# An FFN's last output group: its weights moved into activation room, four norms moved behind the loop, and residual rows queued behind chunks

## The chip, the cores and the metric

The kernel runs on one core of one Trainium2 chip. The metric is the device time of one execution in microseconds, lower is better. The time given is the median of several runs.

## The reference

Two layers over a sequence of 1024 positions with 1024 channels, all in float32. Layer 0 mixes tokens with a state-space model and a gated linear unit, layer 1 with a short gated convolution. Each layer then has a dense SwiGLU FFN and an embedding that is gated by the residual stream:

```python
h = x
for i in range(2):
    hn = rmsnorm(h, norm_mix_g[i])
    mix = s5_mixer(hn, ...) if i % 2 == 0 else shortconv_mixer(hn, ...)
    h = h + mix
    h = h + swiglu_ffn(rmsnorm(h, norm_ffn_g[i]), ffn_w_in[i], ffn_w_out[i])
    gate = sigmoid(rmsnorm(h, norm_ple_g[i]) @ ple_w_gate[i])
    h = h + gate * (p[i] @ ple_w_up[i])
return rmsnorm(h, final_norm_g)
```

The FFN's hidden width is 2816, which is 22 pieces of 128. `swiglu_ffn` is `(silu(gate) * up) @ w_out` with `gate, up` from `u @ w_in`.

## The kernel before, in words

The sequence is cut into 8 tiles `t` of 128 positions. Each product of two float32 matrices is made from three products of a rounded high part and a low part (`mm3`, lines 121 to 124): high by high, high by low, low by high. `split` (lines 86 to 88) makes the two parts, the high one with a cast on ScalarE (ACT), the low one with a subtract on VectorE (DVE). A weight piece or an activation tile thus fills two parts of a room.

The rooms are: `ulow`, which is cut in four quarters `q`, each with two weight rooms (`slot_low(q, s)`), or the normed activations of tiles `q` and `q + 4` (`act_view`); `uhigh` with six weight rooms (`slot_high(i)`); and the tile pool `s8` with four more (`slot_new(i)`), two of which also serve as the place of a normed row `xn` in `norm_tile`. Everything that is loaded from memory and then split or multiplied goes through four raw slots of 512 KB, `r0` to `r3`, taken in turn by `raw_tile`: raw weights, chunks of hidden activations and, where norms come in pairs, normed rows.

The FFN's first half, `ffn_in`, writes the hidden activations to memory (`hid`). Its second half is `ffn_out`, which lists a room for each of the 22 pieces of the output weights, cuts them into three groups of 8, 8 and 6, and calls `out_phase`. `out_phase` also makes the convolution's output product (`conv_out`, two groups of four pieces). Its work:

- Group 0's weights are fetched ahead. Then, group by group, all tiles follow in the order 0, 4, 1, 5, 2, 6, 3, 7 (`ORDER`).
- For each tile the chunks of hidden activations are loaded on the queue of the sync engine (SP), four pieces to a chunk (line 346). In group 0 the tile's residual row `h[t]`, 512 KB, is loaded there too (line 348).
- For each half of the 1024 output columns, each piece has three matmuls of 512 columns. A tile has 48 in a group of 8 pieces, 36 in a group of 6, 24 in the convolution. The sum is added to `h[t]` on DVE (line 360); in the last group its square sum is taken on ACT (line 139).
- After a tile, one fetch of the next group's weights is made if its room is free already (the flag that stands with the room). Fetches whose room is still in use are made after the whole loop. In the last group the fetches are those of the gate's weights (`ple_units`).
- In the last group `last_post(t)` follows the tile. In an FFN that is `norm_tile`: norm, 8 transposes on TensorE, and two splits into the tile's place in `ulow`. For the convolution it is the function in `posted` that calls `norm_pair(q)` for tiles `q` and `q + 4`, pair 0 after tile 1, pair 1 after tile 2, pair 2 after tile 3, pair 3 after tile 7, and spills the rows to memory on the queue of GpSimd (POOL). A pair is two multiplies (line 173), 16 transposes (line 181), four differences and seven splits.

After an FFN's output stage comes `ple`, the gate: two halves of the columns, each over all tiles in the same order, 24 matmuls a tile. After the convolution's output stage comes the second FFN's `ffn_in`, whose first product takes the first block of all four pairs.

The instructions of each engine are put in order by a planner when the program is built. It goes by the order in which the program is written, among what its own model finds ready; `first()` raises a few instructions by 100 places. On the chip each engine and queue runs its list in that order.

Of the kernel before, what the change touches and what calls it, by code (L numbers as in the profile page):

```python
# [9 lines left out]
F32 = mybir.dt.float32  # L10
# [13 lines left out]
def trunk(  # L24
# [7 lines left out]
    nc = tc.nc  # L32
# [31 lines left out]
    HT = T // 2  # L64
# [4 lines left out]
    h, hpool = {}, None  # L69
# [9 lines left out]
    hdram = dram.tile([T, P, D], F32, name="hd")  # L79
    hid = [dram.tile([T, P, 4, 2, P], F32, name=f"hid{i}") for i in range((NHT + 3) // 4)]  # L80

    def psum(pool=None):
        pool = pool or mm
        return pool.tile([P, 512], F32, name="ps" + pool.name, tag="ps")
# [7 lines left out]
    def raw_tile(i=None, shape=(P, D), dt=F32, name="raw"):  # L92
        if i is None:
            slots.append(slots.pop(0))
        tag = slots[-1] if i is None else f"r{i}"
        return (uhp if tag == "r3" else rawp).tile(list(shape), dt, name=name, tag=tag)

    def load_raw(src, pattern, **kw):
        raw = raw_tile()
        nc.sync.dma_start(out=raw.rearrange(pattern, **kw), in_=src)  # L100
        return raw


    def slot_low(q, s):
        v = ulow[:, q, s * 2 * D:(s + 1) * 2 * D].rearrange("p (l n) -> p l n", l=2)
        return v[:, 0], v[:, 1]

    def slot_high(i):
        v = uhigh.rearrange("p c k l j -> p (c k l j)")[:, i * 2 * D:(i + 1) * 2 * D].rearrange("p (l n) -> p l n", l=2)
        return v[:, 0], v[:, 1]  # L110
# [5 lines left out]
    def unit_of(slot, raw):  # L116
        hi, lo = slot
        split(hi, lo, raw)
        return hi, lo

    def mm3(ps, ahi, alo, bhi, blo, start, stop, more=False):
        PE.matmul(ps, ahi, bhi, start=start, stop=False, skip_group_check=more)  # L122
        PE.matmul(ps, ahi, blo, start=False, stop=False, skip_group_check=more)  # L123
        PE.matmul(ps, alo, bhi, start=False, stop=stop, skip_group_check=more)  # L124
# [4 lines left out]
    def first():  # L129
        return tc.high_priority(offset=100)  # L130

    def square(t, cs):

        if "ms" not in squares:
            squares["ms"] = tiny.tile([P, T, 4], F32, name="ms", tag="ms")
        got = squares.setdefault(t, [])
        junk = t2_tile("junk", BF16, D)
        ms = squares["ms"][:, t, len(got):len(got) + 1]
        A.activation(junk[:, cs], h[t][:, cs], AF.Square, scale=1.0 / math.sqrt(D), accum_out=ms)  # L139
        got.append(ms)  # L140
# [13 lines left out]
    def load_gain(g_row):  # L154
        gb = tiny.tile([P, D], F32, name="gb", tag="gb")
        nc.gpsimd.dma_start(out=gb, in_=g_row.partition_broadcast(P))
        return gb
# [49 lines left out]
    def norm_pair(q, gb):  # L207
        t0, t1 = q, q + HT
        halves = 2 if q == HT - 1 else 1
        x0, x1 = normed(t0, gb, halves), normed(t1, gb, halves)  # L210

        def put(c, src):
            split(moving_part(c, 0, q), moving_part(c, 1, q), by_kt(src))

        p11, p12, p22 = transposed(x0, 0), transposed(x1, 0), transposed(x1, 1)
        p21 = transposed(x0, 1, mm)
        put(0, p11)
        b12 = t2_tile("b12")
        A.copy(b12, p12)
        T1 = t2_tile("T1")  # L220
        V.tensor_tensor(T1, b12, p11, ALU.subtract)
        T2 = t2_tile("T2")
        V.tensor_tensor(T2, p22, T1, ALU.subtract)
        put(1, T2)
        put(2, T1)
        put(3, p21)
        T3 = t2_tile("T3")
        V.tensor_tensor(T3, p22, b12, ALU.subtract)
        put(4, T3)
        put(5, p22)  # L230
        T4 = t2_tile("T4")
        V.tensor_tensor(T4, p21, T2, ALU.subtract)
        put(6, T4)
# [92 lines left out]
    def out_phase(wout, groups, last_post, following=()):  # L326


        def fetch(ht, room):
            return unit_of(room(), load_raw(wout[ht], "p n -> p n"))  # L330

        units = {ht: fetch(ht, room) for ht, room, _ in groups[0]}
        for gi, group in enumerate(groups):
            last = gi == len(groups) - 1
            todo = [(early, lambda ht=ht, room=room: units.__setitem__(ht, fetch(ht, room)))
                    for ht, room, early in ([] if last else groups[gi + 1])]
            todo = todo or list(following)
            soon, late = [f for early, f in todo if early], [f for early, f in todo if not early]
            for t in ORDER:
                parts = {}  # L340
                for ht, *_ in group:
                    if ht // 4 not in parts:
                        parts[ht // 4] = ch = raw_tile(shape=(P, 4, 2, P), dt=F32R, name="ch")
                        of = [x[0] % 4 for x in group if x[0] // 4 == ht // 4]
                        ks = slice(min(of), max(of) + 1)
                        nc.sync.dma_start(out=ch[:, ks].bitcast(F32), in_=hid[ht // 4][t, :, ks])
                if gi == 0:
                    nc.sync.dma_start(out=h[t], in_=hdram[t])
                ps = [psum() for _ in range(2)]
                for j in parts:  # L350
                    mine = [x[0] for x in group if x[0] // 4 == j]
                    for nb in range(2):
                        cs = slice(nb * 512, (nb + 1) * 512)
                        for ht in mine:
                            ch = parts[j][:, ht % 4]
                            bhi, blo = (w[:, cs] for w in units[ht])
                            mm3(ps[nb], ch[:, 0], ch[:, 1], bhi, blo, ht == group[0][0], ht == group[-1][0])
                        if mine[-1] == group[-1][0]:
                            with first():
                                V.tensor_tensor(h[t][:, cs], ps[nb], h[t][:, cs], ALU.add)  # L360
                                if last:
                                    square(t, cs)
                if soon:
                    soon.pop(0)()
                if last:
                    last_post(t)
            for f in soon + late:
                f()

    def room_low(q, s):  # L370
        return lambda: slot_low(q, s)

    def room_high(i):
        return lambda: slot_high(i)

    def room_new(i):
        return lambda: slot_new(i)
# [18 lines left out]
    def ffn_out(l, post, following):  # L396
        rooms = [(room_low(q, s), False) for s in range(2) for q in range(HT)]
        rooms += [(room_high(i), True) for i in range(6)] + [(room_new(i), True) for i in range(4)]
        rooms += [(room_high(i), False) for i in range(4)]
        hts = [(ht, *room) for ht, room in enumerate(rooms)]  # L400
        cuts = [0, 8, 16, NHT]
        out_phase(ffn_w_out[l].rearrange("(ht p) n -> ht p n", p=P), [hts[a:b] for a, b in zip(cuts, cuts[1:])], post,
                  following)

    def ple_units(l, nb, rooms):

        wg = ple_w_gate[l].rearrange("(kt p) n -> p kt n", p=P)
        units = {}

        def fetch(u):  # L410
            raw = load_raw(wg[:, 2 * u:2 * u + 2, nb * 512:(nb + 1) * 512], "p (kt n) -> p kt n", kt=2)
            units[u] = [a.rearrange("p (kt n) -> p kt n", kt=2) for a in unit_of(rooms[u](), raw)]

        return units, [lambda u=u: fetch(u) for u in range(KT // 2)]
# [595 lines left out]
    def posted(gain, pairs):  # L1010

        gb = load_gain(gain)

        def pair(q):
            norm_pair(q, gb)
            spill(q)
            spill(q + HT)

        def post(t):
            if not pairs:  # L1020
                return norm_tile(t, gb)
            if 0 < t < HT:
                pair(t - 1)
            if t == T - 1:
                pair(HT - 1)
        return post
# [17 lines left out]
        h_tiles()  # L1044

    def ffn_ple(l, last):
        units, makers = ple_units(l, 0, [room_high(i) for i in (4, 5, 0, 1)])
        ffn_out(l, posted(norm_ple_g[l], False), [(i < 2, f) for i, f in enumerate(makers)])
        if last:
            gb = load_gain(final_norm_g)  # L1050
            ple(l, units, lambda t: final_tile(t, gb))
        else:
            ple(l, units, posted(norm_mix_g[l + 1], True))
# [46 lines left out]
```

## Time and profile before

| | us |
|---|---|
| median of 3 runs (2353.3 to 2358.04) | 2356.06 |
| the profiled execution | 2359.43 |
| its span, first to last instruction | 2357.5 |
| PE busy | 2247.0 (95%) |
| DVE busy | 1331.9 (56%) |
| ACT busy | 765.5 (32%) |
| POOL busy | 163.1 (7%) |
| mean granted clock of TensorE | 0.981 |

PE is TensorE's matmuls, PEld its weight loads, L346 is line 346 of the kernel. In a row of waits stand what waited, for what, the total in us, how often, and the longest. In a row of the timeline stand start, length, engine, line, operation, out<-in, shape and count, and in brackets the idle time before it with what ended it. In a row of the chain stand start, length and what was on it. Matmuls overlap, so one that the timeline shows with 0.39 us leaves room for the next after some 0.23. In the stage order of the span: state-space mixer and gated unit to about 420 us, first FFN's first half to 848, its output stage to 1113, gate to 1226, convolution's first half to about 1460, its output stage to 1557, second FFN's first half from 1571 to 1998, its output stage to 2260, last gate and final norm to the end.

### The profile page before, as it was taken

The page shows a single profiled execution, that of the slowest core. Times are in us where ns is not written, and L with a number is a line of the kernel's source. Part 1 is how long each engine was busy: PE and PEld are TensorE (multiplying, and loading weights), DVE is VectorE, ACT ScalarE, POOL GpSimd, SP SyncE. Part 2 cuts the span into 40 slices and gives each one's busy share as a digit, 9 for nine tenths or more (in the row PEclk, how much of TensorE's full clock was granted, in tenths as well). Part 3 has the DMA queues.
Part 4 walks back from the last instruction along what each step waited for, and adds up shares of the span by engine and source line. Part 5 has one row for each costly group of instructions (what it writes and reads, how often), then busy time and mean ns, then how long its engine had stood idle before and what let it go on. Part 6 is the DMA issues. An engine that isn't in the chain of part 4 may idle for free.

```text
span 2357.5 us, 27090 instructions
## 1 busy us (share of the span) xinstructions
PE 2247.0 (95%) x10253; PEld 1835.7 (78%) x10253; DVE 1331.9 (56%) x2246; ACT 765.5 (32%) x1449; POOL 163.1 (7%) x268
## 2 busy tenths in 40 slices
PE   6888999899999999999979999989999999999998
PEld 4776887788888878878858888768888888788787
DVE  7785326866666642125488776487666666121454
ACT  6554223433333320013343332153333333000232
POOL 2110001000000000000000000010000001000000
PEclk8999999999999999999989999999999999999999
DMA  7555202333333364333232225434333335543333
GB/s 246 141 135 148 69 1 89 105 112 112 111 114 110 107 241 149 118 127 114 70 129 81 90 92 179 159 125 125 108 108 107 111 113 172 212 139 107 108 109 110
DMA packets 212978, 288.87 MB, mean 123 GB/s; under 512 B 21360, under 2 KB 152432, under 8 KB 212848
## 3 DMA queue, kind: packets, MB, share of 16 engines
q1 hardware_dynamic: 191520, 212.63, 29.0%
q0 software_dynamic: 20928, 74.47, 10.2%
q8 instruction: 80, 1.31, 0.2%
q14 instruction: 50, 0.41, 0.1%
q10 hardware_dynamic: 400, 0.04, 0.0%
HBM read 190.93 MB, written 79.69 MB: 115 GB/s over the span
## 4 chain that ended last, share of the span: by engine, by line
PE 85%; DMA 6%; DVE 5%; ACT 1%; SPq 1%; issue 1%; POOL 0%; DVEq 0%; POOLq 0%; ACTq 0%
PE psmm L122 27%; PE psmm L124 27%; PE psmm L123 27%; DMA ch<-hid 2%; PE pstr L181 1%; DMA raw<-in_ffn_w_out_dram 1%; DMA tw<-tmp 1%; DVE W L575 1%; DVE gv L925 1%; DMA h<-hd 1%; DVE tmp L575 1%; DVE ulow L88 1%; DVE uhigh L88 1%; PE pstr L874 0%; DVE raw L575 0%
## 5 line engine op out<-in xcount | busy, mean ns | idle before, releaser
L122 PE MATMUL psmm<-ulow,ws 128*128 128x512 f32 x896 | 351.1, 393 | 1.6 <-ACT s L301 1.6
L123 PE MATMUL psmm<-ulow,ws 128*128 128x512 f32 x896 | 350.6, 391 | 0.0
L124 PE MATMUL psmm<-ulow,ws 128*128 128x512 f32 x896 | 350.4, 391 | 0.0
L124 PE MATMUL psmm<-uhigh,ws 128*128 128x512 f32 x672 | 265.3, 395 | 0.0
L122 PE MATMUL psmm<-uhigh,ws 128*128 128x512 f32 x672 | 265.1, 394 | 0.0
L123 PE MATMUL psmm<-uhigh,ws 128*128 128x512 f32 x672 | 264.9, 394 | 0.0
L360 DVE TENSOR_TENSOR h<-psmm,h 128x512 f32<-128x512 f32 x128 | 88.0, 690 | 276.6 <-PE psmm L124 276.6
L88 DVE TENSOR_TENSOR ws<-raw,ws 128x512 fp32r<-128x512 f32 x224 | 153.6, 688 | 117.8 <-ACT ws L87 117.4
L87 ACT CAST ws<-raw 128x512 fp32r<-128x512 f32 x224 | 137.5, 619 | 213.0 <-PE psmm L124 211.2
L122 PEld LDWEIGHTS psmm<-ulow,ws 128*128 128x128 f32 x896 | 169.4, 189 | 39.5 <-ACT s L301 2.9
L123 PEld LDWEIGHTS psmm<-ulow,ws 128*128 128x128 f32 x896 | 169.4, 189 | 36.2
L124 PEld LDWEIGHTS psmm<-ulow,ws 128*128 128x128 f32 x896 | 169.2, 189 | 36.2
L87 ACT CAST ws<-st 128x512 fp32r<-128x512 f32 x168 | 104.0, 620 | 204.4 <-PE psmm L124 189.5
L123 PEld LDWEIGHTS psmm<-uhigh,ws 128*128 128x128 f32 x672 | 126.1, 188 | 30.3
L124 PEld LDWEIGHTS psmm<-uhigh,ws 128*128 128x128 f32 x672 | 126.1, 188 | 30.3
L122 PEld LDWEIGHTS psmm<-uhigh,ws 128*128 128x128 f32 x672 | 126.1, 188 | 29.1
L323 POOL DMA_DIRECT2D hid<-hs x104 | 78.2, 755 | 903.4 <-DVE hs L88 895.4
L122 PE MATMUL psmm<-ulow,ch 128*128 128x512 f32 x320 | 128.4, 401 | 10.8 <-DMA ch<-hid 10.8
L139 ACT ACTIVATE junk<-h 128x512 bf16<-128x512 f32 (+1 forms) x113 | 64.0, 567 | 204.0 <-DVE h L360 104.0
L87 ACT CAST uhigh<-raw 128x1024 fp32r<-128x1024 f32 x36 | 37.2, 1049 | 278.9 <-PE psmm L124 136.7
L123 PE MATMUL psmm<-ulow,ch 128*128 128x512 f32 x320 | 127.6, 399 | 0.0
L124 PE MATMUL psmm<-ulow,ch 128*128 128x512 f32 x320 | 127.5, 398 | 0.0
(240 smaller groups left out, 4238.5 us busy)
## 6 DMA issues: line engine op xcount, KB each, us to landing
hid<-hs POOLq DMA_DIRECT2D x104, 512.0 KB, 4.3
ch<-hid SPq DMA_DIRECT2D x96, 512.0 KB, 3.7
raw<-in_ffn_w_in_dram SPq DMA_DIRECT2D x88, 512.0 KB, 4.4
raw<-in_ffn_w_out_dram SPq DMA_DIRECT2D x44, 512.0 KB, 3.6
hd<-h POOLq DMA_DIRECT2D x24, 512.0 KB, 3.0
h<-hd SPq DMA_DIRECT2D x24, 512.0 KB, 8.7
raw<-in_conv_w_in_dram SPq DMA_DIRECT2D x24, 512.0 KB, 4.0
up<-ev SPq DMA_DIRECT2D x32, 256.0 KB, 3.2
```

Source lines behind the costliest of these rows:

```text
L87: A.copy(hi, src)
L88: V.tensor_tensor(lo, src, hi.bitcast(F32), ALU.subtract)
L122: PE.matmul(ps, ahi, bhi, start=start, stop=False, skip_group_check=more)
L123: PE.matmul(ps, ahi, blo, start=False, stop=False, skip_group_check=more)
L124: PE.matmul(ps, alo, bhi, start=False, stop=stop, skip_group_check=more)
L139: A.activation(junk[:, cs], h[t][:, cs], AF.Square, scale=1.0 / math.sqrt(D), accum_out=ms)
L181: PE.transpose(pt[:, c * P:(c + 1) * P], xn[:, kt * P:(kt + 1) * P], ident)
L323: nc.gpsimd.dma_start(out=hid[ht // 4][half * HT:(half + 1) * HT, :, ht % 4].rearrange("t p l j -> p t l j"), in_=hs.bitcast(F32))
L360: V.tensor_tensor(h[t][:, cs], ps[nb], h[t][:, cs], ALU.add)
L575: V.tensor_tensor(o, a, b, op)
L925: V.tensor_tensor_scan(gv[:, g, 1:P], dec, sv[:, g, 1:P], 0.0, ALU.mult, ALU.add)
```

## The change

There are four edits.

1. In group 0, a residual row's load is tied behind the last chunk load of its tile in the queue of SP (`tc.issue_after`). This holds for both FFNs and the convolution.
2. The last four of the FFN's 22 weight pieces go to the low rooms of quarters 2 and 3 in place of `slot_high(0..3)`. Group 0 has left these rooms before group 1 begins, so all six fetches of the last group are marked early.
3. Since these rooms are also the place of the normed tiles 2, 6, 3 and 7, the last group calls `last_post` only for tiles 0, 4, 1 and 5; the other four follow after all groups, in the same order. The test stands in `out_phase`, so it holds for the convolution too: pair 0 stays after tile 1, pairs 1, 2 and 3 follow after the loop.
4. The gate's four weight units go to `slot_high(0..3)` in place of 4, 5, 0, 1, and all four are marked early.

```diff
         units = {ht: fetch(ht, room) for ht, room, _ in groups[0]}
+        kept = []
         for gi, group in enumerate(groups):
...
-                        nc.sync.dma_start(out=ch[:, ks].bitcast(F32), in_=hid[ht // 4][t, :, ks])
+                        load = nc.sync.dma_start(out=ch[:, ks].bitcast(F32), in_=hid[ht // 4][t, :, ks])
                 if gi == 0:
-                    nc.sync.dma_start(out=h[t], in_=hdram[t])
+                    with tc.issue_after(load.ins):
+                        nc.sync.dma_start(out=h[t], in_=hdram[t])
...
-                if last:
+                if last and t % HT < HT // 2:
                     last_post(t)
+                elif last:
+                    kept.append(t)
             for f in soon + late:
                 f()
+        for t in kept:
+            last_post(t)
...
         rooms += [(room_high(i), True) for i in range(6)] + [(room_new(i), True) for i in range(4)]
-        rooms += [(room_high(i), False) for i in range(4)]
+        rooms += [(room_low(q, s), True) for q in (2, 3) for s in range(2)]
...
-        units, makers = ple_units(l, 0, [room_high(i) for i in (4, 5, 0, 1)])
-        ffn_out(l, posted(norm_ple_g[l], False), [(i < 2, f) for i, f in enumerate(makers)])
+        units, makers = ple_units(l, 0, [room_high(i) for i in range(4)])
+        ffn_out(l, posted(norm_ple_g[l], False), [(True, f) for f in makers])
```

## The prediction

> **What bounds the kernel now.** I read the page first, then the waits of the matmul engine, then a table of stretches, and last the queue of the sync engine and the chain of work at each place where the table showed lost time.
>
> ```profile
> span 2357.5 us, 27090 instructions
> PE 85%; DMA 6%; DVE 5%; ACT 1%; SPq 1%; issue 1%; POOL 0%; DVEq 0%; POOLq 0%; ACTq 0%
> ch<-hid SPq DMA_DIRECT2D x96, 512.0 KB, 3.7
> h<-hd SPq DMA_DIRECT2D x24, 512.0 KB, 8.7
> ```
>
> TensorE is the bound: 85% of the chain that ended last is its work. A change that removes no matmul can win only where TensorE stands still. Its waits say where that is.
>
> ```profile
> PE pstr L181 <- DVE xn L173: 36.0, 5, 10.7
> PE psmm L122 <- DMA ch<-hid: 19.9, 7, 4.6
> ```
>
> Two waits matter: transposes that wait for a normed row (36.0 us in 5 waits, at the ends of stages that norm pairs) and matmuls that wait for a chunk of hidden activations (19.9 us in 7). The change touches the second, and, through the convolution's output stage, the first.
>
> The next rows are stretches of the span. After the length come busy time and instructions of PE, PEld, DVE, ACT and POOL, the granted clock, and DMA share and GB/s.
>
> ```profile
> 848.02:880.00 31.98, 27.39 (x109) 21.81 (x109) 9.23 (x12) 3.33 (x5) 2.05 (x3) 0.89 0.80 301
> 880.00:1030.00 150.00, 150.00 (x653) 122.49 (x652) 30.57 (x37) 10.40 (x10) 0.00 (x0) 1.00 0.38 126
> 1036.00:1054.00 18.00, 13.23 (x45) 9.86 (x44) 6.52 (x8) 4.48 (x7) 0.56 (x1) 0.81 0.42 145
> 1112.59:1158.09 45.50, 45.50 (x201) 37.00 (x200) 20.13 (x33) 16.76 (x32) 2.12 (x2) 1.00 0.32 104
> 1465.00:1485.00 20.00, 17.27 (x73) 13.38 (x72) 8.68 (x12) 4.17 (x5) 1.65 (x3) 1.00 0.89 326
> 1485.00:1523.00 38.00, 38.00 (x164) 30.58 (x163) 13.32 (x21) 3.34 (x9) 2.24 (x4) 1.00 0.35 119
> 1557.15:1571.31 14.16, 3.44 (x25) 3.10 (x23) 11.32 (x20) 6.50 (x14) 1.44 (x2) 0.73 0.48 149
> 1997.65:2029.00 31.35, 27.90 (x114) 22.16 (x113) 8.00 (x11) 3.36 (x5) 2.06 (x3) 0.95 0.79 303
> 2184.00:2202.00 18.00, 13.21 (x48) 10.01 (x47) 6.51 (x8) 4.48 (x7) 0.56 (x1) 0.81 0.44 153
> ```
>
> The second row is undisturbed: 150.00 us for 653 matmuls, 0.230 us each at full clock. With that price each disturbed stretch gives its loss, slow restart included:
> - start of the first FFN's output stage: 31.98 - 109 x 0.230 = 6.9 us
> - its step from group 1 to group 2: 18.00 - 45 x 0.230 = 7.7
> - start of the convolution's output stage (price 38.00 / 164 = 0.232, from the row after it): 20.00 - 73 x 0.232 = 3.1
> - start of the second FFN's output stage: 31.35 - 114 x 0.230 = 5.1
> - its step from group 1 to group 2: 18.00 - 48 x 0.230 = 7.0
>
> Together 29.8 us. The step from group 2 to the gate (1112.59) shows no loss: PE busy is the whole stretch.
>
> **Part 1: residual rows behind the chunks.** The queue of the sync engine at the first start, and the chain there:
>
> ```profile
> 849.34 3.57 SPq L348 DMA_DIRECT2D h<-hd  x6
> 853.94 1.59 SPq L346 DMA_DIRECT2D ch<-hid  x2
> 859.44 0.33 SPq L100 DMA_DIRECT2D raw<-in_ffn_w_out_dram  x1
> ```
> ```profile
> 853.94 15.60 DMA ch<-hid
> 869.58 0.80 PE psmm L122
> ```
>
> Six residual rows are issued from 849.34, as nothing holds them back. The chunk issued at 853.94 (the second of the second tile, which waited for its raw slot) lands 15.60 us later instead of the usual 3.7, and the matmul starts at 869.58. With the change only the first tile's row stands ahead of it, and the second tile's row is behind it: it lands near 853.94 + 3.7 = 857.6, or 862.6 with the 8.7 us that rows take in the loaded queue. TensorE stood still for 31.98 - 27.39 = 4.6 us of that stretch, so the matmul that stopped needed it at 865.0. The stall goes by either latency. Same order, same cure at the other two starts. Each start can keep all of its loss or none; I take none, gain 6.9 + 3.1 + 5.1 = 15.1.
>
> What is late next: the rows themselves, 24 DMAs, each now behind two chunks (one in the convolution). A tile's last chunk is issued when a slot comes free, about halfway through the tile before it (853.94 is 5.9 us into the first tile's 48 x 0.230 = 11.0); the row follows within a microsecond, lands by 8.7 us later, and is first needed when 36 of a tile's 48 matmuls are done: 24 x 0.230 + 36 x 0.230 = 13.8 us after issue. Cover 5 us in the FFNs. In the convolution the chunk is issued one tile (24 matmuls, 5.6 us) ahead and the row is needed 12 matmuls into the tile: 8.3 us against 3.7 to 8.7, about even; a lateness of 0.4 us only holds a PSUM buffer. Cost 0.
>
> **Part 2: last group's weights in low rooms.** The chain at the first step from group 1 to 2:
>
> ```profile
> 1026.82 3.56 DMA raw<-in_ffn_w_out_dram
> 1033.29 4.54 DMA raw<-in_ffn_w_out_dram
> 1040.19 5.42 DMA ch<-hid
> 1045.66 0.80 PE psmm L122
> 1046.45 0.43 PE psmm L123
> ```
>
> The four late fetches take all four raw slots; each waits for a chunk of group 1's end to leave, and group 2's chunks wait for them. Row 1040.19 is the chunk that stops TensorE. With the rooms in the low part, free since group 0, the four fetches become early ones. What moves per FFN: 4 DMAs on the sync queue, 4 casts on ACT, 4 subtracts on DVE, into tiles 3 to 6 of group 1, as group 0 has them in every tile with no loss after its start (the 880.00 row holds both). Two gate fetches move from the end of group 2 into its third and fourth tile, with the same DMA, cast and subtract each. These hide beside 36 to 48 matmuls. Without them the chunks rotate as in group 0, so the stall goes: 7.7 + 7.0 = 14.7 us. Ends: 0 if another slot chain delays the chunks, 14.7.
>
> Here the slow restart is part of the price: after the gap the first matmul takes 0.80 and the next 0.43. In the four FFN stretches TensorE idles 4.6, 4.8, 3.5 and 4.8 us (length less busy), 17.7 of a loss of 26.7; the other 9.0 are four restarts of some 2.3. The Trainium skill ("TensorE: Matmul & The Clock Gate", Part 1: The HAM clock gate) says that TensorE falls to half speed after an idle window of about 3.4 us and needs about 3.4 us of work to come back. By that, a restart costs about 1.7 us (an estimate from that page), 6.8 for the four, and the change would gain some 2 us less than the sum has it. The trace agrees in kind: the granted clock of these stretches is 0.81 to 0.95.
>
> **Part 3: four norms of each FFN come after group 2.** Tiles 2, 6, 3, 7 are normed when their room has been read for the last time.
>
> ```profile
> L87 ACT CAST ulow<-pstr x44: 565/587/600, 375.5 to 2272.9; 128x512 fp32r<-128x512 f32 x44
> L88 DVE TENSOR_TENSOR ulow<-pstr,ulow x44: 675/684/692, 376.3 to 2273.6; 128x512 fp32r<-128x512 f32 x44
> ```
>
> Per tile: one multiply on DVE (1.28 us, row 1527.66 below), 8 transposes, 2 casts, 2 subtracts, one power on POOL. DVE: 4 x (1.28 + 2 x 0.68) = 10.6 us. They lie beside the gate's first four tiles, 96 matmuls, which use tiles 0, 4, 1, 5 normed as now: 96 x 0.230 = 22.1 us. DVE is busy 20.13 of 45.50 us in the gate's row above, so 22.1 us leave 12.3 free, and the last norm is needed only after seven such tiles, at 38.6 us. TensorE runs the same 32 transposes in either place. Cost 0; if the cover failed, see the last rival.
>
> **Part 4: the convolution gets the deferral too,** though its last group doesn't use the low rooms. Its norms come in pairs: pair 0 stays, pairs 1 and 2 now follow the loop with pair 3.
>
> ```profile
> 1527.66 1.28 DVE L173 SCALAR_TENSOR_TENSOR xn<-h,rs,gb 128x1024 f32<-128x1024 f32 x1
> 1534.30 0.68 DVE L88 TENSOR_TENSOR uhigh<-pstr,uhigh 128x512 fp32r<-128x512 f32 x1
> 1534.90 0.68 DVE L88 TENSOR_TENSOR uhigh<-T,uhigh 128x512 fp32r<-128x512 f32 x1
> ...
> 1558.30 0.69 DVE L221 TENSOR_TENSOR T<-b,pstr 128x512 f32<-128x512 f32 x1 [0.42 <-ACT b L219]
> ...
> 1565.26 0.69 DVE L275 TENSOR_TENSOR st<-raw 128x512 f32<-128x512 f32 x1 [1.83 <-DMA raw<-in_ffn_w_in_dram]
> ...
> 1568.88 1.42 DVE L173 SCALAR_TENSOR_TENSOR xn<-h,rs,gb 128x512 f32<-128x512 f32 x2 [0.46 <-POOL rs L148]
> ```
> ```profile
> 1537.63 0.60 PE L181 MATMUL pstr<-ident,xn 128*128 128x128 f32 x4
> 1569.69 1.97 PE L181 MATMUL pstr<-ident,xn 128*128 128x128 f32 x8 [10.71 <-DVE xn L173]
> ```
> ```profile
> 1543.55 0.87 PE pstr L181 x8
> ```
>
> Tile 1's row was normed at 1527.66, but transposed only at 1537.63, after tile 2's matmuls, which stand ahead of the pair in the program. So transposes aren't drawn ahead of earlier matmuls, and in the changed kernel those of pairs 1, 2 and 3 all come after the last matmul (1557.15). The pair's raw slots say the same: pair 2's second row takes the slot of the last chunk. Now only the rest of pair 2 (from 1558.30) and pair 3 lie there, in a gap of 14.16 us with only 25 instructions on TensorE. Added on DVE, at 0.60 from start to start (1534.30 to 1534.90): pair 1's 4 differences and 7 subtracts, 6.6; pair 2's second multiply, 1.2, and its two subtracts that now come earlier, 1.2; pair 3's first multiply, 1.4. Sum 10.4. Off: 24 transposes leave the busy matmul time for the gap, 24 x 0.109 (0.87 / 8) = 2.6; the weight row's wait (1.83) is covered by the longer work, 1.8. Net +6.0. Ends: -2.6 if all of the added work finds holes; +14 if nothing is covered and the weight rows, whose slots pair 2 now holds, come some 4 us later still. I take 6.0, since the rows show DVE nearly continuous there. POOL's six row spills of these pairs wait only for their rows; cost 0.
>
> **Sum.** -15.1 - 14.7 + 0 + 6.0 = -23.8 us. The profiled execution took 2359.43 us with a span of 2357.5, which would become 2333.7; it lies 3.4 above the median of the runs shown, 2356.06. From the median: 2332.
>
> **Rivals.**
> - The convolution's tail costs nothing, as DVE and ACT have room during tiles 2, 6, 3, 7: 2356 - 29.8 = 2326. Against it: the transposes' order.
> - The starts don't improve, since raw slots and not rows hold the chunks: 2356 - 14.7 + 6.0 = 2347. For it: chunks do wait for slots. Against: 15.60 us in flight.
> - The tail costs 14 or more: 2356 - 29.8 + 14 = 2340.
> - Slower: at the end of group 2 the four norms stand in TensorE's queue ahead of the gate's matmuls, one after the other, each multiply, transposes, cast, subtract: 1.28 + 0.87 + 0.59 + 0.68 = 3.4 us, four of them 13.7, with a slow restart of 2.3, 16 in each FFN: 2356 - 23.8 + 32 = 2364. It decides from 12 us in each FFN. Against it: no loss at 1112.59 now, where the last tile's norm is in the same place.
> - The rows or weights don't move in the issued order at all: 2356.
>
> **How the numbers follow.** Forecast 0.53, free tail 0.13, starts unimproved 0.11, dear tail 0.13, slower 0.06, no change 0.04. A difference under 0.2% (4.7 us) can't be told from none. Faster 0.89, same 0.05, slower 0.06. The range runs from 2322 (free tail and some microseconds of restart saved) to 2347.
>
> **What would show it.** Right: no wait of a matmul for a chunk at the three starts and two steps; chunks landing in about 4 us at the starts; rows queued one per tile; a longer wait of transposes at the convolution's end, with 16 or more transposes after the last matmul. Wrong: a wait of the gate's matmuls for normed tiles, or of a DVE add for its row, or a tail that differs by over 8 us from now.

## The result

The changed kernel takes 2331.6 us (median of 4 runs, 2329.59 to 2333.13) against 2355.07 for the kernel before (4 runs, one more than the table above has). The ratio is 0.9899, with a 95% interval of 0.9881 to 0.9916, so it is 23.5 us or 1.0% faster. The forecast was 2332, in a range of 2322 to 2347.

The profiled execution took 2333.13 us with a span of 2331.4. Lines of its page, and the longest waits of TensorE, to set against those of before:

```profile
span 2331.4 us, 27095 instructions
PE 89%; DVE 5%; DMA 3%; ACT 1%; issue 1%; SPq 1%; POOL 0%; DVEq 0%; POOLq 0%; ACTq 0%
ch<-hid SPq DMA_DIRECT2D x96, 512.0 KB, 4.1
h<-hd SPq DMA_DIRECT2D x24, 512.0 KB, 5.7
```
```profile
PE pstr L181 <- DVE xn L173: 25.3, 4, 10.4
...
PE pstr L181 <- ACT b L219: 6.7, 2, 5.3
...
PE psmm L122 <- ACT ws L87: 2.2, 1, 2.2
```

The wait of a matmul for a chunk (19.9 us in 7 waits before) is gone from the list. DMA's share of the chain fell from 6% to 3%. Rows land in 5.7 us instead of 8.7. New are the waits for the copy `b` (line 219) and for `ws`, both at the convolution's end. They replace the one wait of 10.7 us for `xn` there.

Three stretches account for the whole gain. Each row here gives its length, PE busy with instructions, granted clock, DMA share and GB/s. The first and third row run from an FFN output stage's first matmul to the gate's second half; the second from the convolution's output stage to that of the second FFN. Before:

```profile
848.02:1158.09 310.07, 300.71 (x1313) 0.98 0.41 138
1454.35:1997.65 543.30, 529.63 (x2321) 0.99 0.42 130
1997.65:2305.98 308.33, 299.52 (x1314) 0.98 0.40 138
```

After:

```profile
845.19:1141.24 296.05, 296.05 (x1314) 1.00 0.43 144
1437.54:1984.04 546.50, 534.50 (x2322) 0.98 0.42 129
1984.04:2279.81 295.77, 295.77 (x1313) 1.00 0.43 144
```

In both FFNs TensorE now never stands still, as busy time equals the length, and the clock is 1.00. They gain 14.0 and 12.6 us; the convolution loses 3.2. The sum is -23.4 us, which is the difference of the medians. The two spans differ by 26.1; the other 2.8 lie ahead of 848, in the state-space stage, which none of the edits touches. Over the kernels shown here, the start of the first FFN's output stage lay anywhere between 842.4 and 849.2 us, so spans alone can't tell apart what differs by less than about 5 us.

### The profile page after: what moved, and what is told of

It is laid out like the page before. It is cut to its first block, busy times and chain, and to the rows that moved or that the text cites. A ratio compares the mean times of both kernels' runs of the same rounds, so it can differ in the third digit from the quotient of the medians.

```text
span 2331.4 us, 27095 instructions
## 1 busy us (share of the span) xinstructions
PE 2245.9 (96%) x10253; PEld 1835.3 (79%) x10253; DVE 1333.6 (57%) x2246; ACT 768.0 (33%) x1449; POOL 161.2 (7%) x268
## 3 DMA queue, kind: packets, MB, share of 16 engines
q0 software_dynamic: 20928, 74.47, 10.4%
## 4 chain that ended last, share of the span: by engine, by line
PE 89%; DVE 5%; DMA 3%; ACT 1%; issue 1%; SPq 1%; POOL 0%; DVEq 0%; POOLq 0%; ACTq 0%
PE psmm L122 28%; PE psmm L124 28%; PE psmm L123 28%; PE pstr L181 1%; DMA tw<-tmp 1%; DVE gv L931 1%; DVE W L581 1%; DVE ulow L88 1%; DVE tmp L581 0%; PE pstr L946 0%; PE pstr L880 0%; PE pstr L948 0%; PE pstr L947 0%; DMA h<-in_x_dram 0%; DVE sv L581 0%
## 5 line engine op out<-in xcount | busy, mean ns | idle before, releaser
L123 PE MATMUL psmm<-ulow,ch 128*128 128x512 f32 x448 | 177.2, 396 | 0.0
L122 PE MATMUL psmm<-ulow,ch 128*128 128x512 f32 x448 | 176.9, 395 | 0.1
L124 PE MATMUL psmm<-ulow,ch 128*128 128x512 f32 x448 | 176.8, 395 | 0.0
L88 DVE TENSOR_TENSOR ws<-st,ws 128x512 fp32r<-128x512 f32 x168 | 115.2, 686 | 2.4 <-ACT ws L87 2.2
```

The lines of the kernel that those rows point to most:

```text
L88: V.tensor_tensor(lo, src, hi.bitcast(F32), ALU.subtract)
```

## The experiments

The table gives each kernel's median, its ratio to the kernel before, and the length of the three stretches, found in each trace by the same first matmuls.

| run | median us | ratio (95%) | FFN 1 | conv. | FFN 2 |
|---|---|---|---|---|---|
| before | 2355.07 | | 310.1 | 543.3 | 308.3 |
| after | 2331.60 | 0.9899 (0.9881 to 0.9916) | 296.1 | 546.5 | 295.8 |
| rows_only | 2342.16 | 0.9947 (0.9935 to 0.9960) | 301.6 | 541.1 | 302.8 |
| no_rows | 2344.87 | 0.9962 (0.9948 to 0.9975) | 301.7 | 549.1 | 301.2 |
| defer_only | 2354.72 | 1.0004 (0.9995 to 1.0013) | 307.5 | 543.1 | 308.3 |
| late_gate | 2331.49 | 0.9903 (0.9889 to 0.9918) | 296.1 | 545.9 | 295.7 |
| conv_in_loop | 2328.13 | 0.9889 (0.9876 to 0.9903) | 295.8 | 541.8 | 296.0 |
| raised | 2333.81 | 0.9909 (0.9896 to 0.9922) | 296.0 | 548.3 | 296.0 |
| raised_psum | 2330.30 | 0.9898 (0.9883 to 0.9913) | 296.0 | 545.2 | 296.0 |
| after_psum | 2332.76 | 0.9906 (0.9891 to 0.9920) | 296.0 | 546.6 | 295.8 |
| rows_pool | 2351.58 | 0.9983 (0.9973 to 0.9994) | 303.5 | 547.2 | 301.8 |
| psum_junk | 2323.08 | 0.9872 (0.9855 to 0.9888) | 296.0 | 538.5 | 296.0 |

Each ratio is against the kernel before on the same chip in the same session, where its median was between 2354.56 and 2355.54.

**The rows alone** (rows_only), on the kernel before:

```diff
-                        nc.sync.dma_start(out=ch[:, ks].bitcast(F32), in_=hid[ht // 4][t, :, ks])
+                        load = nc.sync.dma_start(out=ch[:, ks].bitcast(F32), in_=hid[ht // 4][t, :, ks])
...
-                    nc.sync.dma_start(out=h[t], in_=hdram[t])
+                    with tc.issue_after(load.ins):
+                        nc.sync.dma_start(out=h[t], in_=hdram[t])
```

> The kernel before with the first edit alone: each residual row tied behind its tile's last chunk, weights and norms as before. Theory (rows in flight hold up the chunk behind them): the chunk waits at the three starts go, 6.9 + 3.1 + 5.1 us, and the two steps from group 1 to 2 keep their 7.7 and 7.0; 2355 - 15 = 2340. Rival (the raw slots, not the rows, hold the chunks): 2355, with the waits still there.

It is 13.4 us faster by medians; the stretches, each from one trace, give 8.5 + 2.2 + 5.5 = 16.2. The waits for chunks fell from 19.9 us in 7 to 9.5 in 3, which are the two steps from group 1 to 2:

```profile
PE psmm L122 <- DMA ch<-hid: 9.5, 3, 4.4
```

So rows in flight, not slots, held up the chunks at the starts.

**Everything but the rows** (no_rows):

```diff
-                    with tc.issue_after(load.ins):
-                        nc.sync.dma_start(out=h[t], in_=hdram[t])
+                    nc.sync.dma_start(out=h[t], in_=hdram[t])
```

> The changed kernel without the first edit: residual rows issued as freely as before, the weights in the low rooms and the deferred norms kept. Theory (the edits add up): 2331.6 + 15 = 2347, waits at the starts back, none at the steps from group 1 to 2. Rival (without the late fetches the chunks are early enough that the rows don't matter, so the edits overlap): below 2340.

It takes 2344.9 us, 13.3 above the changed kernel, which is what rows_only gains on the kernel before. By medians the two parts add up and don't overlap.

```profile
PE psmm L122 <- DMA ch<-hid: 10.5, 4, 3.8
```

The four waits are those of the three starts (two of them in the convolution); none is at a step from group 1 to 2.

**The FFN's deferral alone** (defer_only), on the kernel before; `following` is empty in the convolution:

```diff
+        kept = []
...
-                if last:
+                if last and (t % HT < HT // 2 or not following):
                     last_post(t)
+                elif last:
+                    kept.append(t)
...
+        for t in kept:
+            last_post(t)
```

> The kernel before with the FFN's deferral alone: norms of tiles 2, 6, 3, 7 behind all groups, the weights in their old rooms, rows as before, the convolution's pairs in the loop. Theory (the first four gate tiles cover the norms): 2355, no wait of the gate's matmuls. Rival (the norms stand in the way of the gate, 13.7 us of serial norm work with a slow restart in each FFN): up to 2355 + 32 = 2387; a partial stall shows as some microseconds in the gate's first half.

No difference by medians. Norms behind the loop cost nothing where the gate's first tiles cover them.

**The gate's rooms and flags as before** (late_gate), on the changed kernel:

```diff
-        units, makers = ple_units(l, 0, [room_high(i) for i in range(4)])
-        ffn_out(l, posted(norm_ple_g[l], False), [(True, f) for f in makers])
+        units, makers = ple_units(l, 0, [room_high(i) for i in (4, 5, 0, 1)])
+        ffn_out(l, posted(norm_ple_g[l], False), [(i < 2, f) for i, f in enumerate(makers)])
```

> The changed kernel with the fourth edit undone: the gate's weights in high rooms 4, 5, 0, 1 and the last two fetched after group 2 as before. Theory (this edit earns nothing of its own, as the step into the gate showed no loss before): 2331.6 within 2. Rival (the two late fetches, in line with the raw slots and the four deferred norms, stop the gate's first matmuls): 2335 or more, with a wait of the gate's first tile for its weights.

The same time, and the same stretches within 0.6 us. The fourth edit earns nothing by itself.

**The convolution's pairs in the loop again** (conv_in_loop), on the changed kernel:

```diff
-                if last and t % HT < HT // 2:
+                if last and (t % HT < HT // 2 or not following):
```

> The changed kernel with the deferral for the FFNs alone: the convolution's pairs 1 and 2 are normed inside the loop again. Theory (pair 1's differences and splits and part of pair 2's were pushed behind the last matmul): the convolution's end is as it was before, 6 us shorter than in the changed kernel; 2331.6 - 6 = 2325.6. Rival (what DVE and ACT do at the end is set by the second FFN's weights and costs the same either way): 2331.6.

2328.13 us; its four runs (2327.71 to 2328.68) all lie below all four of the changed kernel. So the deferral costs 3.5 us by medians and 4.8 by the stretch (546.5 - 541.8). Without the rows edit it is 6.0 (no_rows against defer_only, 549.1 - 543.1). The cost is real; its size came out a little under the expected 6.

**What makes it cost** was tried in three steps. First (raised), the transposes of the deferred pairs are moved up in the planner's order:

```diff
+        with first() if raised else nullcontext():
             for c in range(KH):
                 ...
...
+        raised.extend([] if following else kept)
         for t in kept:
             last_post(t)
+        raised.clear()
```

> The changed kernel with one thing more: the transposes of the convolution's three deferred pairs are raised by 100 places in the planner's order, so pair 1's stand among the matmuls of the loop's last two tiles. Theory (the place of the transposes in TensorE's list is what pushes pair 1's DVE work behind the end): pair 1's 11 DVE operations, 6.6 us, run before the last matmul, the end shrinks by 4 to 7, 2326 to 2328. Rival (the weights' raw slots and DVE's order alone set the end): 2331.6 within 1.5.

No gain: 2333.8. Transposes on TensorE, where the line is now 183, and the copy and the last square sum on ACT:

```profile
1526.01 0.60 PE L183 MATMUL pstr<-ident,xn 128*128 128x128 f32 x4
1531.57 1.03 PE L183 MATMUL pstr<-ident,xn 128*128 128x128 f32 x8
...
1540.95 0.80 PE L183 MATMUL pstr<-ident,xn 128*128 128x128 f32 x4 [1.92 <-ACT b L221]
```
```profile
1539.70 0.63 ACT L140 ACTIVATE junk<-h 128x512 bf16<-128x512 f32 x1
1540.24 0.19 ACT L140 ACTIVATION_READ_ACCUMULATOR junk<-h 128x1 f32 x1
1540.33 0.56 ACT L221 COPY b<-pstr 128x512 f32<-128x512 f32 x1
```

Pair 1 is transposed at 1526 and 1531.57, in the loop, as meant. But the copy that its differences need runs at 1540.33, right behind the last tile's square sum. The unused output `junk` of the square sums and the copy `b12` take tiles of one ring of five, `t2`, in the order of the program.

Second (raised_psum), the square sums of this stage write their unused output into the PSUM tile that has just been added (`square` gets the place as a third argument), and third (after_psum) the same without the raised transposes:

```diff
-                                    square(t, cs)
+                                    square(t, cs, None if following else ps[nb])
```

> The run with raised transposes, and the square sums of the convolution's output stage write their unused output into the finished PSUM tile in place of a tile of the ring t2. In the raised run pair 1 was transposed at 1532, but its first copy ran at 1540, behind the last tile's square sums, whose unused outputs take the same five-tile ring t2 ahead of it. Theory (two orders in a row hold pair 1's DVE work behind the end: the transposes' place, then the ring): now 6 to 7 us of it run before the last matmul; 4 to 7 us under the raised run, 2327 to 2330. Rival (DVE's own order and the weights' slots set the end): 2332 to 2334, as in the raised run.

> The changed kernel with the same square sums written into PSUM, transposes not raised. Theory: the transposes still stand behind the last matmul, so the ring alone changes little; 2331.6 within 2. Rival (the ring alone was the cause): 2325 to 2328.

```profile
1530.18 0.57 ACT L221 COPY b<-pstr 128x512 f32<-128x512 f32 x1
...
1539.73 0.60 ACT L140 ACTIVATE psmm<-h 128x512 f32<-128x512 f32 x1 [1.67 <-DVE h L364]
```

With both, the copy comes at 1530.18, 9.6 us ahead of the last square sum, and the second FFN's first product starts 108.8 us after the output stage's first matmul (1436.93 to 1545.74) instead of 111.9 (1437.54 to 1549.45). With PSUM alone the convolution's stretch stays at 546.6. So transposes and ring stand in a row, and both must go before pair 1's work moves into the loop. Yet the whole gains only 3.5 us on raised and 1.3 on the changed kernel, within the intervals. What the earlier start gains is in part given back behind it: the first product's second and third matmul wait for low parts that DVE makes (the first two rows), and the second product waits for its weights:

```profile
1547.81 0.79 PE L123 MATMUL psmm<-ulow,ws 128*128 128x512 f32 x1 [1.27 <-DVE ulow L88]
1549.61 0.80 PE L124 MATMUL psmm<-ulow,ws 128*128 128x512 f32 x1 [0.15 <-DVE ws L88]
1556.47 1.31 PE L122 MATMUL psmm<-ulow,ws 128*128 128x512 f32 x2 [2.57 <-ACT ws L87]
```

The convolution's stretch in three parts, by the starts in the timelines (us):

| kernel | output stage, first to last matmul | gap to the next FFN's first product | from there to that FFN's output stage |
|---|---|---|---|
| before | 102.8 | 14.2 | 426.3 |
| conv_in_loop | 99.6 | 14.9 | 427.3 |
| after | 97.0 | 14.9 | 434.6 |
| raised_psum | 99.5 | 9.3 | 436.4 |

The deferral shortens the first part by the 24 transposes that leave it (2.5 us), leaves the gap as it was, and costs 7.3 us behind the first product. raised_psum has the gap shorter by 5.6, but the third part stays long.

What remains between raised_psum and conv_in_loop (545.2 - 541.8 = 3.4 us) wasn't isolated by a run. The traces point to DVE's list. The first part again, in conv_in_loop, after and raised_psum, and last the time behind raised_psum's first product:

```profile
1437.07:1536.64 99.57, 99.57 (x451) 80.93 (x450) 57.31 (x92) 25.69 (x54) 11.76 (x19) 1.00 0.52 197
1437.54:1534.57 97.03, 97.03 (x427) 78.36 (x426) 47.84 (x77) 21.43 (x46) 11.45 (x19) 1.00 0.56 200
1436.93:1536.47 99.54, 99.54 (x451) 80.87 (x450) 53.36 (x85) 26.08 (x55) 11.44 (x19) 1.00 0.54 196
1545.74:1562.29 16.55, 12.22 (x29) 8.15 (x29) 16.55 (x29) 8.12 (x15) 0.00 (x0) 0.60 0.23 68
```

The deferral moves 15 DVE operations (9.5 us) behind the last matmul, and raised_psum brings back 8 of them. Behind its first product DVE is busy for all of 16.55 us, and from its last matmul to the end of these 16.55 us neither TensorE nor DVE nor ACT waits for a weights' load. So the loads, whose raw slots the deferred pairs hold longer, don't set this end; that the other 7 operations cost the 3.4 us is likely, but not shown.

**Rows on another queue** (rows_pool), on the kernel before:

```diff
-                    nc.sync.dma_start(out=h[t], in_=hdram[t])
+                    nc.gpsimd.dma_start(out=h[t], in_=hdram[t])
```

> The kernel before with the residual rows loaded on POOL's queue instead of SP's, all eight as early as their room allows, nothing else changed. It tells apart why a chunk behind six rows lands late. Theory A (it is the order within one queue): the chunk no longer stands behind the rows, lands in 4 to 8 us, and most of the 15 us at the starts go: 2340 to 2345. Theory B (it is the bytes in flight, whatever the queue): chunks land as late as before, 2355.

3.8 us faster, between the two theories. Times from issue to landing of the chunks near the first start, min, median and max, before (846 to 866 us):

```profile
L346 SPq DMA_DIRECT2D ch<-hid x4: 319/320/320, 849.0 to 865.0; - x4
DMA to landing us min/median/max: 6.2/12.0/15.6
```

with the rows on POOL's queue (840 to 866 us):

```profile
L346 SPq DMA_DIRECT2D ch<-hid x5: 319/320/326, 841.3 to 856.6; - x5
DMA to landing us min/median/max: 7.4/7.9/8.9
```

and in the changed kernel (843 to 866 us):

```profile
L347 SPq DMA_DIRECT2D ch<-hid x5: 319/319/1718, 845.3 to 865.6; - x5
DMA to landing us min/median/max: 3.4/6.1/8.9
```

In the one queue a chunk waited for all rows ahead of it, up to 15.6 us: the row issued last before that chunk, at 852.6, landed at 867.8, and the chunk at 869.5. From two queues the transfers share the engines: no chunk takes over 8.9, but none is under 7.4. The chunk issued at 843.7 landed at 851.6, ahead of four of the six rows that POOL had issued from 838.7 to 841.4. The FFNs, with 11 us a tile, gain 6.6 each. The convolution, with 5.6 us a tile, loses 3.9: its waits for chunks are 5.2 us in 2, against 2.7 in 2 before, and DVE waits 3.1 us for rows there, which it did not before. The Trainium skill ("DMA: Bandwidth & Descriptors", Queues, rings and completion order) says that each DMA engine takes turns between the queues that have work, a packet at a time. The landing at 851.6 agrees with that. The run changes one thing more: on POOL's queue the first rows leave at 838.7, on SP's at 846.9, so the shorter times aren't the queue's alone. Rows taken early still do harm from the other queue; holding each back behind its tile's chunks gains more (13.4 us against 3.8).

**A version that beats both** (psum_junk): the changed kernel with the convolution's pairs in the loop (the edit of conv_in_loop), and the unused square outputs of the stages that norm pairs in PSUM:

```diff
-                                    square(t, cs)
+                                    square(t, cs, None if following else ps[nb])
...
-                        square(t, hc)
+                        square(t, hc, ps)
...
-                    square(t, cs)
+                    square(t, cs, ps[:, 0:256])
```

> A version that may be faster than both: the changed kernel with the deferral for the FFNs alone, and the unused square outputs of the three stages that norm pairs (gated unit, first gate, convolution's output) in PSUM. Theory (at these ends the last tile's square sum waits in the ring behind the pair before it): each of the three ends, with waits of 10 to 12 us for a normed row now, shrinks by 2 to 4; 2328 - 9 = 2319. Rival (the wait moves to the pair's other work on DVE): 2328 within 2.

2323.08 us, ratio 0.9872. Of the three ends only the convolution's became shorter, by 3.3 us (538.5 against 541.8). At the other two the longest waits for `xn` stayed at 10.4 and 11.5 us (10.4 and 10.5 in conv_in_loop), so the ring isn't what sets them. The other 2.6 us between the traces lie ahead of the gated unit's end, in the stage whose length varies; nothing shows that the edit earns them. It is the fastest kernel here: its four runs (2322.67 to 2327.34) all lie below those of conv_in_loop.

## Why the prediction was right

- **Starts (Part 1).** Forecast 15.1 us; 13.4 (rows_only) and 13.3 (no_rows against after) by medians, 16.2 and 13.6 by stretches. The mechanism is shown from both sides. The rows came in time: no wait for a row stands among the waits of TensorE or of DVE's adds. Chunks at the first start took 3.4 to 8.9 us, not about 4 as the forecast's sign had it; no matmul waited for them.
- **Steps (Part 2).** Forecast 14.7 for both FFNs. no_rows has this part without the rows and gains 8.4 + 7.1 = 15.5 in the two FFN stretches against the kernel before, 12.9 against defer_only; on top of the rows (rows_only to after) it is 12.6. Starts and steps of the FFNs together, with the slow restarts, were forecast at 26.7 and gave 26.6.
- **FFN norms (Part 3).** Forecast 0, measured 0 (defer_only), and busy time equals the length in both FFN stretches of the changed kernel. The rival with the norms in the gate's way is out.
- **Convolution (Part 4).** Forecast +6.0. Measured +3.5 by medians, +4.8 to +6.0 by stretches. The sign and the step that the transposes come behind the last matmul are right, and so is the added work, 10.4 us forecast in 15 operations and 9.5 measured:

```profile
1534.41 1.47 PE L181 MATMUL pstr<-ident,xn 128*128 128x128 f32 x12
...
1545.08 1.11 PE L181 MATMUL pstr<-ident,xn 128*128 128x128 f32 x4 [5.29 <-ACT b L219]
1547.66 1.97 PE L181 MATMUL pstr<-ident,xn 128*128 128x128 f32 x8 [1.46 <-DVE uhigh L88]
1549.45 0.79 PE L122 MATMUL psmm<-ulow,ws 128*128 128x512 f32 x1
...
1559.71 0.50 PE L122 MATMUL psmm<-ulow,ws 128*128 128x512 f32 x1 [2.23 <-ACT ws L87]
```
```profile
1534.57:1549.45 14.88, 7.00 (x45) 5.49 (x42) 14.84 (x25) 8.85 (x18) 1.50 (x2) 0.81 0.32 105
1549.45:1566.00 16.55, 12.58 (x35) 9.00 (x35) 16.23 (x28) 9.23 (x18) 0.00 (x0) 0.66 0.24 66
```

The same 16.55 us behind the first product in the kernel before:

```profile
1571.31:1587.86 16.55, 16.33 (x67) 13.07 (x66) 15.07 (x26) 11.01 (x21) 0.00 (x0) 0.92 0.33 97
```

The place of the loss is not as forecast. The added DVE work, less the covered wait, was put into the gap ahead of the next FFN's first product. That gap grew only from 14.16 to 14.88 us: DVE is busy 14.84 of it, where it was busy 11.32 before, so the gap's idle time took up part of the work. The first weight row was cast 6.7 us behind the last matmul (8.1 before), so it didn't come late. The rest shows behind the first product: 35 instructions on TensorE where there were 67, a wait of 2.23 us for the second product's weights, and a clock of 0.66. A sign failed too: the longest wait of transposes at this end fell from 10.7 to 5.3 us. And the cause named, the transposes' place alone, was only the first of two that hold pair 1's work back: moving them (raised) gained nothing while the ring `t2` held the copy, and with both gone most of the cost still stands. So this part was right in kind and wrong in place, and it is luck that its size came out close: forecast was a longer gap, and measured (against conv_in_loop) 7.3 us behind the first product, less 2.5 for the transposes that left the loop. The whole would have stayed in its range with any value from 3.5 to 6.0.

- **Rivals.** "Starts don't improve", "slower by norms in the gate" and "no change" are excluded by rows_only, defer_only and the result. "Free tail" and "dear tail" lie on either side of the 3.5 to 6.0 measured.

## What to carry to other kernels

Price a stall in the stretch where it stands, as length less matmuls at the clean rate of a neighbouring stretch; so the slow restart of TensorE is counted, and the prices add up. A load that nothing holds back is not free: in an in-order queue it goes ahead of the load that matters next, and tying it behind that one cost nothing here and gave 13 us. When a function is shared by stages, ask what an edit does in each: the deferral was free where 22 us of matmuls covered it, and cost 3.5 us or more in the convolution, whose next stage needs all pairs at once.

## What the runs showed of the hardware

Two queues don't order each other's transfers: chunks that stood behind rows in one queue took up to 15.6 us, chunks beside rows of another queue 7.4 to 8.9, one of them landing ahead of rows that were issued before it. Rows there took longer in turn (median 10.4 us over the kernel with rows on POOL's queue, against 8.7 before and 5.7 after). Square sums on ACT that write their unused result to PSUM took 0.60 us (raised_psum) against 0.63 to SBUF in bf16 (raised), so PSUM was no dearer a place for it.
